# RoPE with scaled positions on one core: storing unit 0 from its fp16 tile by four casting DMAs, without ScalarE's copies

## The chip, the cores and the metric

One core of a Trainium2 chip. The metric is the device time of one execution in microseconds (us); a kernel's time is the median of its runs. "Span" is the length of the one profiled execution, which is some 1.7 us shorter than the timed figure. All runs quoted here are in the fast state. Each ratio is the mean time of one kernel's fast runs over the mean of the other's in the same rounds, so it is not quite the ratio of the medians beside it. A transfer (DMA) is carried by 16 DMA engines in packets, here mostly one row of one partition each; the trace keeps a record of every packet (start, duration, bytes), and on each engine one of 4 bytes that reports the completion of a DMA.

## The reference

```python
x: (8, 8, 1024, 64) float32; freqs: (32,); positions: (1024,); scale 0.5
angles = np.outer(positions * scale, freqs)
cos, sin = np.cos(angles), np.sin(angles)
x_first, x_second = x[..., :32], x[..., 32:]
out_first  = x_first * cos - x_second * sin
out_second = x_first * sin + x_second * cos
return np.concatenate([out_first, out_second], axis=-1).astype(np.float32)
```

16.8 MB of fp32 are read and 16.8 MB of fp32 are written. Little arithmetic stands against these bytes.

## The kernel before

The 64 (batch, head) pairs are four units of 16; a unit is a tile of 128 partitions by N = 8192 elements, that is 4 MB of fp32 or 2 MB of fp16. NH is half a row. Units are loaded by GpSimd's queue, which casts fp32 to fp16 on the way (half of unit 0 comes as fp32 by SyncE's and ScalarE's queues, to start early). VectorE computes in fp16, in place; ScalarE copies each half unit to an fp32 tile; units 0 and 1 are stored by GpSimd's queue, units 2 and 3 by SyncE's.

```python
# loads on GpSimd's queue (fp32 in memory, fp16 tiles); unit 0's second half was loaded above
pin(nc.gpsimd.dma_start(out=Xf[0][:, :NH], in_=xv[0][:, :NH]))
# ... constants ...
for u in range(1, NU):
    c = C2 if u == NU - 1 else 0                      # C2 = 1024: the last load is split
    pin(nc.gpsimd.dma_start(out=Xf[u][:, : N - c], in_=xv[u][:, : N - c]))
    if c:
        pin(nc.gpsimd.dma_start(out=Xf[u][:, N - c :], in_=xv[u][:, N - c :]))
# ... table of sin and cos (T), by TensorE and ScalarE; cut ...
for u in range(NU):
    OUT = xout.tile([P, N], FP32, tag="O")            # three buffers
    for s in range(2):                                # halves of the row
        # ... pr = Xs * sin; Xs = Xs * cos; Xs.first -= pr.second; Xs.second += pr.first (VectorE)
        pin(nc.scalar.copy(out=OUT[:, ns], in_=Xf[u][:, ns]))
        if u >= NU // 2:
            pin(nc.sync.dma_start(out=ov[u][:, ns], in_=OUT[:, ns]))
    if u < NU // 2:
        c = C1 if u == 0 else 0                       # C1 = 512
        if c:
            pin(nc.gpsimd.dma_start(out=ov[u][:, :c], in_=OUT[:, :c]))
        pin(nc.gpsimd.dma_start(out=ov[u][:, c:], in_=OUT[:, c:]))
```

## Time and profile before

| | before |
|---|---|
| time, median of 3 runs | 84.4 us (84.38 to 84.5) |
| span | 82.7 us |
| VectorE busy | 60.3 us (73%) |
| ScalarE busy | 40.1 us (49%) |
| memory read and written | 16.79 + 16.78 MB |

The prediction below shows the slices, queues, stretches and waits. Two groups of the page belong to the change. The columns are line, engine, operation, output<-input with its shape, count; then busy us and mean ns of one; then the engine's idle time before them and what ended it.

```profile
L165 ACT CAST OUT<-X 128x4096 f32<-128x4096 f16 x8 | 28.8, 3605 | 24.2 <-DVE X L162 24.2
...
L172 POOL DMA_DIRECT2D out_dram<-OUT x2 | 1.1, 531 | 20.2 <-ACT OUT L165 20.2
```

The eight copies are the fp32 outputs, 3.6 us each, and all of ScalarE's waits before them are for VectorE. GpSimd's store issues in turn wait for the copies.

### The profile page before, as it was taken

How to read it: one execution, taken by the hardware profiler on the slowest of the kernel's cores; microseconds unless marked ns; L12 is line 12 of the kernel's file. 1: busy time of each engine (PE TensorE's matmuls, PEld its weight loads, DVE VectorE, ACT ScalarE, POOL GpSimd, SP SyncE). 2: the span in 40 equal slices, each digit the busy share in tenths (PEclk: the TensorE clock that was granted, in tenths of full speed). 3: DMA queues.
4: the chain of work that ended last, by engine and by line, in shares of the span. 5: the costliest groups of instructions: out<-in, count | busy, mean ns of one | idle time of the engine just before them, and what ended most of it. 6: DMA issues, size and time to landing. Idle time of an engine off the chain costs nothing.

```text
span 82.7 us, 184 instructions
## 1 busy us (share of the span) xinstructions
PE 6.4 (8%) x18; PEld 2.4 (3%) x18; DVE 60.3 (73%) x40; ACT 40.1 (49%) x18; POOL 5.7 (7%) x16
## 2 busy tenths in 40 slices
PE   0011798200000000000000000000000000000000
PEld 0011232000000000000000000000000000000000
DVE  0306276999999999999999999999999997000000
ACT  0602159999960691294089049309705912950000
POOL 4950000000020002000000200000000000000000
PEclk9999999995555555555555555555555555555555
DMA  3899998996998999999499889989899899999991
GB/s 55 323 323 269 297 325 186 254 254 135 246 254 182 198 254 222 222 222 222 36 456 446 357 386 476 507 357 460 380 523 404 365 428 428 460 404 436 428 428 79
DMA packets 2099, 26.22 MB, mean 317 GB/s; under 512 B 371, under 2 KB 371, under 8 KB 563
## 3 DMA queue, kind: packets, MB, share of 16 engines
q0 software_dynamic: 1088, 15.73, 66.7%
q1 hardware_dynamic: 720, 9.44, 27.3%
q10 hardware_dynamic: 290, 1.06, 3.2%
q14 instruction: 1, 0.00, 0.0%
HBM read 16.79 MB, written 16.78 MB: 406 GB/s over the span
## 4 chain that ended last, share of the span: by engine, by line
DVE 54%; ACT 14%; issue 7%; DMA 6%; PE 5%; DVEq 1%; ACTq 0%
DVE X L158 19%; DVE pr L157 19%; DVE X L162 9%; DMA freq_row<-in_freqs_dram 6%; ACT T L144 5%; DVE X L159 5%; ACT OUT L165 4%; PE ps L134 4%; ACT X L145 4%; DVEq L203 1%; PE cfreq L102 1%; ACT tab L127 1%; DVE r L118 1%; DVE y L109 1%; ACTq L71 0%
## 5 line engine op out<-in xcount | busy, mean ns | idle before, releaser
L165 ACT CAST OUT<-X 128x4096 f32<-128x4096 f16 x8 | 28.8, 3605 | 24.2 <-DVE X L162 24.2
L157 DVE TENSOR_TENSOR pr<-X,T 128x4096 f16<-128x4096 f16 x8 | 18.3, 2292 | 1.0 <-ACT T L144 0.7
L158 DVE TENSOR_TENSOR X<-X,T 128x4096 f16<-128x4096 f16 x8 | 18.3, 2292 | 0.3
L159 DVE TENSOR_TENSOR X<-X,pr 128x2048 f16<-128x2048 f16 x8 | 9.8, 1225 | 0.3
L162 DVE TENSOR_TENSOR X<-pr,X 128x2048 f16<-128x2048 f16 x8 | 9.7, 1218 | 0.0
L144 ACT CAST T<-ps 128x1024 f16<-128x1024 f32 x6 | 5.7, 1030 | 2.6 <-PE ps L134 2.6
L134 PE MATMUL ps<-tab,sel 128*128 128x512 f16 x16 | 5.8, 503 | 2.6 <-ACT tab L127 2.2
L142 DVE CAST T<-ps 128x1024 f16<-128x1024 f32 x2 | 2.4, 1224 | 2.2 <-PE ps L134 2.2
L145 ACT CAST X<-X0f 128x4096 f16<-128x4096 f32 x1 | 3.6, 3650 | 0.0
L100 DVE COPY sel<-one 128x2048 f16<-128x2048 f16 x1 | 0.7, 694 | 2.8 <-POOL one L89 2.8
L122 ACT ACTIVATE tab<-r 128x256 f16<-128x256 f32 x1 | 0.4, 416 | 4.4 <-DVE r L118 4.4
L172 POOL DMA_DIRECT2D out_dram<-OUT x2 | 1.1, 531 | 20.2 <-ACT OUT L165 20.2
L122 ACT ACT_TABLE_LOAD x1 | 1.3, 1283 | 2.1 <-issue 2.1
L134 PEld LDWEIGHTS <-sel 128*128 128x128 f16 x16 | 1.9, 122 | 6.1 <-issue 5.7
L95 POOL DMA_DIRECT2D X<-in_x_dram x3 | 2.0, 658 | 0.0
L171 POOL DMA_DIRECT2D out_dram<-OUT x1 | 0.6, 554 | 19.1 <-ACT OUT L165 19.1
L105 DVE CAST posf<-pos_i 128x8 f32<-128x8 int32 x1 | 0.2, 173 | 2.2 <-DMA pos_i<-in_positions_dram 2.2
L102 PE MATMUL cfreq<-freq_row,coef 1*128 1x32 f32 x2 | 0.6, 391 | 5.9 <-DMA freq_row<-in_freqs_dram 5.9
L109 DVE TENSOR_TENSOR y<-posf,cfreq 128x256 f32<-128x256 f32 x1 | 0.4, 420 | 0.7 <-PE cfreq L102 0.7
L85 POOL DMA_DIRECT2D X<-in_x_dram x1 | 0.7, 669 | 0.8 <-POOLq L189 0.8
L102 PEld LDWEIGHTS cfreq<-freq_row,coef 1*128 1x128 f32 x2 | 0.5, 308 | 5.9 <-issue 5.9
L97 POOL DMA_DIRECT2D X<-in_x_dram x1 | 0.6, 557 | 0.0
(12 smaller groups left out, 2.8 us busy)
## 6 DMA issues: line engine op xcount, KB each, us to landing
out_dram<-OUT SPq DMA_DIRECT2D x4, 2048.0 KB, 11.6
X<-in_x_dram POOLq DMA_DIRECT2D x2, 2048.0 KB, 24.2
out_dram<-OUT POOLq DMA_DIRECT2D x1, 4096.0 KB, 20.4
out_dram<-OUT POOLq DMA_DIRECT2D x1, 3840.0 KB, 21.1
X<-in_x_dram POOLq DMA_DIRECT2D x1, 1792.0 KB, 37.5
X0f<-in_x_dram SPq DMA_DIRECT2D x1, 1024.0 KB, 4.7
X<-in_x_dram POOLq DMA_DIRECT2D x1, 1024.0 KB, 11.5
X0f<-in_x_dram ACTq DMA_DIRECT2D x1, 1024.0 KB, 13.4
```

Of the source, the lines that this page charges most:

```text
L95: pin(nc.gpsimd.dma_start(out=Xf[u][:, : N - c], in_=xv[u][:, : N - c]))
L102: nc.tensor.matmul(out=cfreq, lhsT=coef, rhs=freq_row, start=True, stop=True)
L122: pin(nc.scalar.activation(out=tab[:, 0], in_=r, func=AF.Sin, bias=0.0, scale=-_TWO_PI_DN))
L134: nc.tensor.matmul(out=ps[:, i].rearrange("p t w -> p (t w)"), lhsT=sel[:, g + i].rearrange("s h q -> s (h q)"), rhs=tab.rearrange("s t k ...
L142: pin(nc.vector.tensor_copy(out=dst, in_=ps))
L144: pin(nc.scalar.copy(out=dst, in_=ps))
L145: pin(nc.scalar.copy(out=Xf[0][:, NH:], in_=X0f[:, :NH]))
L157: pin(nc.vector.tensor_tensor(out=pr, in0=Xs, in1=sin_b, op=ALU.mult))
L158: pin(nc.vector.tensor_tensor(out=Xs, in0=Xs, in1=cos_b, op=ALU.mult))
L159: pin(nc.vector.tensor_tensor(out=Xs[:, :, 0, :], in0=Xs[:, :, 0, :], in1=pr[:, :, 1, :], op=ALU.subtract))
L162: pin(nc.vector.tensor_tensor(out=Xs[:, :, 1, :], in0=pr[:, :, 0, :], in1=Xs[:, :, 1, :], op=ALU.add))
L165: pin(nc.scalar.copy(out=OUT[:, ns], in_=Xf[u][:, ns]))
```

## The change

The intent: take unit 0's two copies off ScalarE. GpSimd's queue can cast while it stores, so unit 0 goes from its fp16 tile to fp32 memory directly, in four DMAs of 2048 elements a row (8 KB at the fp32 end).

```diff
--- before.py
+++ after.py
@@ -45,7 +45,6 @@
     K8 = S // P
     G = P // HP
     W = K8 * half
-    C1 = 512
     C2 = 1024
     assert S % HP == 0 and D == 2 * half and NBH % HEADS == 0 and G * K8 == K
 
@@ -145,8 +144,11 @@
     pin(nc.scalar.copy(out=Xf[0][:, NH:], in_=X0f[:, :NH]))
 
 
+
     for u in range(NU):
-        OUT = xout.tile([P, N], FP32, tag="O")
+        OUT = Xf[0]
+        if u:
+            OUT = xout.tile([P, N], FP32, tag="O")
         for s in range(2):
             ks = slice(s * KH, (s + 1) * KH)
             ns = slice(s * NH, (s + 1) * NH)
@@ -162,14 +164,15 @@
             pin(nc.vector.tensor_tensor(
                 out=Xs[:, :, 1, :], in0=pr[:, :, 0, :], in1=Xs[:, :, 1, :], op=ALU.add
             ))
-            pin(nc.scalar.copy(out=OUT[:, ns], in_=Xf[u][:, ns]))
+            if u:
+                pin(nc.scalar.copy(out=OUT[:, ns], in_=Xf[u][:, ns]))
             if u >= NU // 2:
                 pin(nc.sync.dma_start(out=ov[u][:, ns], in_=OUT[:, ns]))
         if u < NU // 2:
-            c = C1 if u == 0 else 0
-            if c:
-                pin(nc.gpsimd.dma_start(out=ov[u][:, :c], in_=OUT[:, :c]))
-            pin(nc.gpsimd.dma_start(out=ov[u][:, c:], in_=OUT[:, c:]))
+            parts = 4 if u == 0 else 1
+            for i in range(parts):
+                c = slice(i * N // parts, (i + 1) * N // parts)
+                pin(nc.gpsimd.dma_start(out=ov[u][:, c], in_=OUT[:, c]))
 
 
 # ---- launch: one core; inputs and outputs as the reference has them ----
```

## The prediction

> **What bounds the kernel now.** I read the page first (slices, queues), then the stretches, then the chain and the waits, to see whether an engine or the transfers set the end. The page's slices and its queue table:
>
> ```profile
> DVE  0306276999999999999999999999999997000000
> ACT  0602159999960691294089049309705912950000
> DMA  3899998996998999999499889989899899999991
> q0 software_dynamic: 1088, 15.73, 66.7%
> q1 hardware_dynamic: 720, 9.44, 27.3%
> q10 hardware_dynamic: 290, 1.06, 3.2%
> HBM read 16.79 MB, written 16.78 MB: 406 GB/s over the span
> ```
>
> DMA stands near 9 from the second slice to the last but one, that is before, beside and after VectorE's row, while ScalarE's row is full of holes. The dips (6, 4) look like idle time, so I looked closer. The stretches (last two columns: DMA share, GB/s):
>
> ```profile
> 17.00:29.00 12.00, 0.00 (x0) 0.00 (x0) 11.72 (x8) 8.39 (x4) 0.55 (x1) 0.58 1.02 218
> 29.00:40.00 11.00, 0.00 (x0) 0.00 (x0) 10.83 (x7) 5.85 (x2) 0.53 (x1) 0.50 1.05 214
> 40.00:43.00 3.00, 0.00 (x0) 0.00 (x0) 2.97 (x3) 1.32 (x1) 0.00 (x0) 0.50 0.98 228
> 43.00:53.00 10.00, 0.00 (x0) 0.00 (x0) 9.86 (x6) 5.89 (x2) 0.53 (x1) 0.50 1.00 430
> 53.00:73.00 20.00, 0.00 (x0) 0.00 (x0) 16.59 (x11) 10.35 (x3) 0.00 (x0) 0.50 1.01 433
> 73.00:81.00 8.00, 0.00 (x0) 0.00 (x0) 0.00 (x0) 0.47 (x1) 0.00 (x0) 0.50 0.99 426
> ```
>
> In windows longer than a packet the share is 1: the dips are packets counted whole at their start. Laying the single packet records of the trace end to end confirms it: from 2.2 to 81.3 us some 16 data packets are always open, one for each engine. The GB/s count the bytes that are written: a casting load writes half of what it reads, so 218 is 436 GB/s at the fp32 end, and the plain stores' 430 to 433 are the same speed. So the fp32 bytes of a packet set its duration, cast or not. The queue table agrees: on q0, 15.73 MB hold 7.34 MB of fp16 from 14.68 MB of fp32, so 23.07 fp32 MB in 66.7% of 16 x 82.7 us, which is 26.1 GB/s for each engine; q1, all plain, has 9.44 MB in 27.3%, 26.1 too.
>
> Is there a second bound close behind? The chain that ended last, and what SyncE and GpSimd waited for:
>
> ```profile
> 65.14 2.30 DVE X L158
> 67.45 0.02 issue
> 67.47 1.22 DVE X L159
> 68.69 1.15 DVEq L203
> 69.84 0.02 issue
> 69.86 3.60 ACT OUT L165
> ```
> ```profile
> SPq L167 <- ACT OUT L165: 71.3, 4, 51.2
> ```
> ```profile
> POOL out_dram L171 <- ACT OUT L165: 19.1, 1, 19.1
> ```
>
> VectorE runs without a hole from 13.4 to 69.8 us, then ScalarE's last copy ends at 73.46 and the last 2 MB store is issued at 73.5. It lands 8.3 us later (smallest value of the fp32 tile's issue-to-landing times), at 81.8. That store alone needs 8 packets per engine x 0.611 us = 4.9 us; an early 1 MB load shows what comes on top: it landed in 4.7 us with 8 x 0.309 = 2.5 us of packets, so 2.2 us. Hence about 73.5 + 7.1 = 80.6 us without a backlog, and the backlog is worth 1.2 us. The end is set by the DMA engines, with the VectorE chain 1.2 us behind.
>
> **What the Trainium skill says.** "DMA: Bandwidth & Descriptors", section "Where 436 GB/s comes from", gives 435 GB/s for the 16 engines; the trace shows 430 to 436, so there is nothing left to win in rate. The same page, "Queues, rings and completion order", says that an engine takes one ring's descriptors in order and turns between rings packet by packet; here unit 0's first piece is issued at 24.3 us but lands 19.3 us later, behind the loads in GpSimd's queue. "Why small descriptors are slow (HBM only)" tells of a fixed overhead per packet; the plain packets here took 0.309 us for 8 KB, 0.611 for 16 KB and 1.213 for 32 KB, some 0.01 us each beyond the bytes. "SBUF — State Buffer", section "Who interferes with whom", says that tensor_tensor does not stall GpSimd's writing of descriptors (marked as inferred); VectorE's products take 2291 to 2293 ns beside all of GpSimd's issues, so I expect no interference.
>
> **The change, part by part.**
>
> *Removed: two ScalarE copies* of 3.605 us (at 20.42 and 27.64), 7.2 of its 40.1 us. Who waited for them? Only GpSimd's two issues of unit 0. ScalarE's next copy, at 34.6, starts when VectorE's L162 is done, and still will. Nothing on VectorE's chain moves: worth 0 directly.
>
> *Moved: the issues of unit 0.* The first two parts can go when VectorE ends the first half, 19.17 + 1.22 = 20.4 us instead of 24.3; the other two at about 27.6 instead of 31.5. But q0 works in order, and in the packet records its last load ends at 42.6; unit 0's first packet started at 42.2. All four parts will queue behind the loads as now: 3.9 us earlier at the issue, 0 at the transfer.
>
> *Moved: buffers.* The output pool has three slots, one held by the early fp32 half of unit 0. Before, unit 3 took unit 0's slot, whose last store landed at 52.6, 10 us before unit 3's first copy at 62.86; afterwards it takes the slot free since 20.5 us. No wait was there, none goes. The second unit's store still waits for its own copies and is issued at 45.6.
>
> *Changed: the packets of unit 0.* This is all that is left on the bound. Before, each engine had 8 packets of 30 KB at 1.138 us and 4 of 4 KB (two 2 KB rows in one) at 0.159: 9.10 + 0.64 = 9.74 us, seen as 42.2 to 52.3. After, four DMAs of 128 rows give 4 x 8 = 32 packets an engine with 8 KB at the fp32 end. At the plain rate of 0.310 us: 9.92 us, +0.18. A cast may add something: casting loads took 1.227 us for 32 KB read against 1.213 plain, 0.014 more; 32 x 0.324 = 10.37 us, +0.63. But in the casting stretch 16.3 packets are open at a time instead of 16.1, so most of the 0.014 overlaps with the next packet. I take +0.25 us. It delays unit 1's packets and, as the backlog never empties, all stores after them up to the last.
>
> *The turn from loads to stores.* Around 39 to 41 us the last load packets take up to 2.24 us instead of 1.076, and the 2 KB ones 0.233 on average instead of 0.173: about 1 us lost for each engine (0.5 + 0.5). I don't know the cause, and the change replaces the small packets just after it; this could go either way by half a microsecond. I leave it at 0.
>
> Sum: 84.4 + 0 + 0 + 0.25 = 84.65, rounded to 84.6 us.
>
> **The rivals.**
> 1. *The casting store is slower than the plain one at the same fp32 bytes.* No casting store is in the profile; only casting loads. If an engine were bound by its elements or by reads of 4 KB, 10% more on 9.7 us would be +1 us (85.4), and slower by 2% (86.1) needs 17%. For it: the direction is untried here. Against it: the loads show the cast hidden at full rate.
> 2. *The earlier issue or the finer rows help*: a shorter turn from loads to stores, up to 1 us, and the floor at 80.6 us caps any such gain at 1.2 us, so 83.2 at best. For it: the lost microsecond at 40 us. Against it: it lies in the loads' packets, which the change leaves alone.
> 3. *ScalarE was a bound and 7.2 us come free.* It idles 24.2 us for VectorE; I give this nothing.
> 4. *Smaller packets on q0 lose their share against SyncE's 16 KB packets.* Queues share by packets, and unit 0 would get less; but unit 0 is through at 52.3 and SyncE's first packet starts at 55.8. And total work is unchanged.
>
> **Range and chances.** The sure term is +0.2, the cast's up to +0.6, the turn plus or minus 0.5: 84.0 to 85.3 us. Faster by over 2% (below 82.7) is beyond the floor unless VectorE's chain itself shortens: 0.02. Slower by over 2% needs casting stores at least 17% slower: 0.07. Within 2%: 0.91.
>
> **What would show it.** Right: VectorE's last L162 still ends near 69.8 us and the last store is issued near 73.5; ScalarE shows 6 copies at 3.605 us, about 33 us busy; GpSimd's first store issue near 20.5; q0 with 320 more packets and about the same share; DMA share still 1.0 from 43 to 81 us, and 420 to 430 GB/s between 43 and 53. Wrong: fewer GB/s in that stretch (rival 1), first stores under way clearly before 42 us or a shorter turn (rival 2), or a VectorE chain that ends earlier, which I have no reason for.

## The result, and the profile after

The changed kernel takes 84.59 us (6 runs, 84.52 to 84.68), the kernel before 84.42 us in the same rounds (6 runs). The ratio is 1.0018, with an interval of 1.0005 to 1.0031: a difference of under 2%, yet a slowdown of about 0.15 us that the interval keeps away from zero.

The page's slices and queue table of the changed kernel (packets, MB, share of 16 engines):

```profile
DVE  0306376999999999999999999999999996000000
ACT  0603169998000000393098059219607903940000
...
DMA  3899997996999899999499999979999799999991
...
q0 software_dynamic: 1440, 15.73, 68.2%
q1 hardware_dynamic: 720, 9.44, 27.3%
q10 hardware_dynamic: 290, 1.06, 3.2%
```

ScalarE's row is now empty in slices 10 to 15, counted from 0, where the two copies were, and DMA's row is as full as before. q0 has 352 more packets: 320 for data (32 instead of 12 on each of 16 engines), and 32 completions, since two more DMAs report from 16 engines each.

The groups that the change touches:

```profile
L168 ACT CAST OUT<-X 128x4096 f32<-128x4096 f16 x6 | 21.6, 3606 | 31.3 <-DVE X L164 31.3
...
L175 POOL DMA_DIRECT2D out_dram<-X x4 | 2.1, 538 | 21.7 <-DVE X L164 21.7
```

Two copies of 3.6 us are gone (28.8 to 21.6), and ScalarE's wait for VectorE grew by 7.1 us (24.2 to 31.3): the freed time became idle time, to the microsecond. The stores now wait for VectorE itself.

The stretches (busy us and instructions of PE, PEld, DVE, ACT and POOL, then the granted clock; the last two columns are DMA share and GB/s written):

```profile
40.00:43.00 3.00, 0.00 (x0) 0.00 (x0) 2.97 (x3) 1.48 (x1) 0.00 (x0) 0.50 0.93 194
43.00:53.00 10.00, 0.00 (x0) 0.00 (x0) 9.86 (x6) 5.73 (x2) 0.53 (x1) 0.50 1.14 440
53.00:73.00 20.00, 0.00 (x0) 0.00 (x0) 16.43 (x11) 10.51 (x3) 0.00 (x0) 0.50 1.00 431
73.00:81.00 8.00, 0.00 (x0) 0.00 (x0) 0.00 (x0) 0.31 (x1) 0.00 (x0) 0.50 1.00 430
```

Unit 0 is written between 42 and 52 us. The share of 1.14 there looks like 14% more work, but the rate fell by only 1%: a casting store of 8 KB is on record for 0.341 us against 0.309 for the plain 8 KB load of before, and the records overlap, with 18 of them open at a time on 16 engines. The share above 1 is an overlap of records and no measure of cost. (440 against 430 is mostly edge: packets are counted whole where they start. With each packet's bytes laid evenly over its record, 44 to 51.5 us has 428 GB/s here and 433 in the kernel before.)

The end of the chain that ended last (start, us, what), and SyncE's wait (us in total, times, longest):

```profile
67.31 1.22 DVE X L161
68.53 1.15 DVEq L206
69.68 0.02 issue
69.70 3.60 ACT OUT L168
```
```profile
SPq L170 <- ACT OUT L168: 71.1, 4, 51.1
```

VectorE's chain is where it was (it ended 0.16 us earlier in this execution, because the frequencies landed earlier), and the last store is issued at 73.3 us. In the packet records unit 1's last packet ends at 65.14 us instead of 65.03, and the last packet of all at 81.55 instead of 81.45. So the delay enters with unit 0 and is carried to the end, although the last store was issued 0.16 us earlier. These are single executions, and the changed kernel's second profile ends at 81.50; the spacing of the packets, shown after the experiments with 2 KB rows, is steadier.

### The profile page after: what moved, and what is told of

The parts are those of the page before. It is cut to its first block, busy times and chain, and to the rows that moved or that the text cites. A ratio compares the mean times of both kernels' runs of the same rounds, so it can differ in the third digit from the quotient of the medians.

```text
span 82.8 us, 184 instructions
## 1 busy us (share of the span) xinstructions
PE 6.5 (8%) x18; PEld 2.5 (3%) x18; DVE 60.3 (73%) x40; ACT 33.0 (40%) x16; POOL 6.7 (8%) x18
## 3 DMA queue, kind: packets, MB, share of 16 engines
q0 software_dynamic: 1440, 15.73, 68.2%
## 4 chain that ended last, share of the span: by engine, by line
DVE 54%; ACT 15%; issue 7%; DMA 5%; PE 5%; DVEq 1%; ACTq 0%
DVE X L160 19%; DVE pr L159 19%; DVE X L164 9%; ACT T L143 6%; DMA freq_row<-in_freqs_dram 5%; DVE X L161 5%; ACT OUT L168 4%; PE ps L133 4%; ACT X L144 4%; DVEq L206 1%; PE cfreq L101 1%; ACT tab L126 1%; DVE r L117 1%; DVE y L108 1%; ACTq L70 0%
## 5 line engine op out<-in xcount | busy, mean ns | idle before, releaser
L168 ACT CAST OUT<-X 128x4096 f32<-128x4096 f16 x6 | 21.6, 3606 | 31.3 <-DVE X L164 31.3
L175 POOL DMA_DIRECT2D out_dram<-X x4 | 2.1, 538 | 21.7 <-DVE X L164 21.7
L175 POOL DMA_DIRECT2D out_dram<-OUT x1 | 0.5, 533 | 16.4 <-ACT OUT L168 16.4
## 6 DMA issues: line engine op xcount, KB each, us to landing
X<-in_x_dram POOLq DMA_DIRECT2D x2, 2048.0 KB, 24.2
```

Of the source, the lines that this page charges most:

```text
L175: pin(nc.gpsimd.dma_start(out=ov[u][:, c], in_=OUT[:, c]))
```

## The experiments

Theory A is the prediction's: the DMA engines are full from 2 to 81 us, a packet costs its bytes at the fp32 end plus a small fixed time, a cast costs nothing, and ScalarE's copies are off the path. The rivals: B, the cast itself costs; C, the freed ScalarE or the earlier issue wins something that fine rows lose again; D, casting loads and casting stores could overlap inside an engine; and one that holds the compute chain to set the end. All kernels below gave correct results. One of the kernel before's eleven runs beside the first four kernels (whole, plain 8 KB, 2 KB, copies kept) took 85.08 us; without it their ratios would be 0.0006 higher.

### One casting store with rows of 32 KB

```diff
-            parts = 4 if u == 0 else 1
+            parts = 1
```

> Unit 0 in one casting store with rows of 32 KB: 8 packets an engine instead of 32. Theory A (the engines are full, a packet costs its fp32 bytes plus about 0.01 us, a cast costs nothing): 0.2 us under the changed kernel, so 84.35 to 84.45, level with the kernel before. Rival B (it is the cast that costs, not the rows): no better than the changed kernel, 84.6 or more. Rival C (the earlier issue wins something and the fine rows lose more): clearly under the kernel before, 84.2 or less.

Measured: 84.5 us, ratio to the kernel before 0.9995 (0.9974 to 1.0017). The same kernel was run again beside the changed kernel itself, unedited:

> The changed kernel once more, unedited, in the same rounds as the next two, so that a few tenths can be compared. Theory A: 84.6, 1.001 to 1.003 of the kernel before.

> The one casting store with rows of 32 KB again, beside the changed kernel: theory A (cost by packets) has it 0.1 to 0.2 us below the changed kernel and level with the kernel before; rival B (cost of the cast) level with the changed kernel.

Measured: the changed kernel 84.51 us, ratio 1.0015 (1.0003 to 1.0028); the single casting store 84.41 us, ratio 0.9995 (0.9982 to 1.0009). Its queue row, from the first of its two runs:

```profile
q0 software_dynamic: 1008, 15.73, 67.1%
```

With the same cast and the same copies gone, but 8 packets an engine instead of 32 and one DMA instead of four, the 0.15 us are gone (in the second call all five runs, 84.33 to 84.46, lie below the changed kernel's five, 84.49 to 84.70). That speaks against B. It also speaks against C: with rows as long as before there should have been a gain, and there is none.

### The old cut, cast

```diff
-            parts = 4 if u == 0 else 1
-            for i in range(parts):
-                c = slice(i * N // parts, (i + 1) * N // parts)
+            cuts = (0, 512, N) if u == 0 else (0, N)
+            for lo, hi in zip(cuts, cuts[1:]):
+                c = slice(lo, hi)
```

> Unit 0 cast in the store, but cut as in the kernel before (512 elements of a row, then the other 7680): the same packets at the fp32 end, 8 of 30 KB and 4 of 4 KB an engine, so the cast alone. Theory A: level with the kernel before within 0.1 us, 84.4 to 84.5. Rival B: like the changed kernel, 84.6.

Measured, in the same rounds as the two above: 84.43 us against 84.45, ratio 1.0002 (0.999 to 1.0015). This is the cast alone, with the kernel before's cut of the rows: it costs nothing that can be measured, at most 0.13 us by the interval. One detail was not as expected: the two 2 KB rows that a plain store puts into one packet stay two packets when they are cast (128 packets of 2 KB in place of 64 of 4 KB).

### Rows of 8 KB without a cast

```diff
-        OUT = Xf[0]
-        if u:
+        if True:
             OUT = xout.tile([P, N], FP32, tag="O")
...
-            if u:
+            if True:
                 pin(nc.scalar.copy(out=OUT[:, ns], in_=Xf[u][:, ns]))
```

> Unit 0 is copied by ScalarE to fp32 as before, and stored without a cast in four DMAs with rows of 8 KB: the row size alone. Theory A: 84.6, like the changed kernel. Rival B (the cast costs): 84.4, like the kernel before. Rival C (earlier issue and free ScalarE win, rows lose): above the changed kernel, 84.8.

Measured: 84.68 us, ratio 1.0018 (0.9994 to 1.0042). Its queue row, and the stretch in which unit 0 is written:

```profile
q0 software_dynamic: 1440, 15.73, 66.9%
```
```profile
43.00:53.00 10.00, 0.00 (x0) 0.00 (x0) 9.83 (x7) 5.42 (x2) 0.53 (x1) 0.50 1.05 445
```

The ratio is the changed kernel's (1.0018), though nothing is cast here and ScalarE works as before. By itself this run cannot tell 84.6 from 84.4, as its interval holds both; with the kernels above it fits the finer cut and not the cast. It also shows how little the queue's share is worth as a measure of cost: the same packets have 66.9% here and 68.2% when they are cast, and the cast kernel is not slower.

### Rows of 2 KB

```diff
-            parts = 4 if u == 0 else 1
+            parts = 16 if u == 0 else 1
```

> Unit 0 in sixteen casting stores with rows of 2 KB: the suspected cost per packet enlarged. Theory A: 64 packets of 4 KB an engine if two rows go into one packet, 52 more than before at 0.009 us, 84.9; 128 packets of 2 KB if they don't, 85.4. Rival B (a cast costs by its bytes): 84.6, like the changed kernel.

Measured: 84.91 us, ratio 1.0044 (1.0022 to 1.0066). Queue row and stretch:

```profile
q0 software_dynamic: 3168, 15.73, 72.6%
```
```profile
43.00:53.00 10.00, 0.00 (x0) 0.00 (x0) 9.86 (x6) 5.71 (x2) 5.30 (x10) 0.50 1.51 438
```

A finer cut costs more, as A has it and B does not. But A's size was wrong. The packets stayed at 2 KB, 128 an engine, for which A expected 85.4. The 116 packets more than before cost 0.0044 x 84.5 = 0.37 us, or 3.2 ns each and not 9. The share of 1.51 shows why the sum of durations misled: each is on record for 0.115 us, but some 1.4 to 1.5 times as many as there are engines are open at a time. The rate did suffer, though the view's 438 hides it by counting unit 1's first packets whole: from 44 to 51.5 us, where unit 0 alone is moved, it is 408 GB/s. GpSimd spent 5.3 us of the stretch on issues; before them it waited for earlier transfers to land.

The packet records show what the cut costs. On each engine, the time from the completion of the last load to that of unit 0's last store (mean of the 16 engines, one profile a kernel unless marked) is:

| unit 0's store | DMAs | packets an engine | us | against before |
|---|---|---|---|---|
| plain, 2 KB + 30 KB rows (before) | 2 | 12 | 9.716 | |
| cast, the old cut | 2 | 16 | 9.698 | -0.02 |
| cast, 32 KB rows (both runs) | 1 | 8 | 9.658 | -0.06 |
| cast, 8 KB rows (the change, both runs) | 4 | 32 | 9.778 | +0.06 |
| plain, 8 KB rows | 4 | 32 | 9.822 | +0.11 |
| cast, 2 KB rows | 16 | 128 | 10.258 | +0.54 |

A cast row costs no more than a plain one: casting packets of 30 KB follow each other every 1.132 us against 1.134 plain, and those of 8 KB every 0.304 against 0.306. The finer cut has two costs, which the times alone do not part. A cast packet is spaced 1207.2 ns at 32 KB, 303.7 at 8 KB and 77.8 at 2 KB, so each packet adds about 2.5 ns to its bytes; and from one completion to the next, a further casting DMA adds 20 ns on each engine (2449.4 ns for the second to fourth part, 2429.5 for the first), a further plain one about 7 (2452.9 against 8 packets at 305.8). From the whole store to the change that is 24 x 2.5 + 3 x 20 = 120 ns, half packets and half DMAs. From unit 0's end to the last packet all are nearly alike: 29.31 us before, 29.33 to 29.40 in the others. The 2 KB kernel's loads happened to be through 0.2 us earlier than the kernel before's in the profiles (42.21 against 42.42 us, mean of the engines), so its 0.37 us, and the 3.2 ns taken from them, are no clean price of a packet.

### ScalarE's copies put back, read by nobody

```diff
-        OUT = Xf[0]
-        if u:
-            OUT = xout.tile([P, N], FP32, tag="O")
+        OUT = xout.tile([P, N], FP32, tag="O")
...
-            if u:
+            if True:
                 pin(nc.scalar.copy(out=OUT[:, ns], in_=Xf[u][:, ns]))
...
-                pin(nc.gpsimd.dma_start(out=ov[u][:, c], in_=OUT[:, c]))
+                pin(nc.gpsimd.dma_start(out=ov[u][:, c], in_=(OUT if u else Xf[0])[:, c]))
```

> The changed kernel with ScalarE's two copies of unit 0 put back; they go to a buffer that nothing reads. Theory A: 84.6, the same as the changed kernel within 0.1 us, ScalarE 40 us busy again. Rival C (7.2 us of ScalarE are worth something): above it by 0.2 us or more.

Measured: 84.64 us, ratio 1.0013 (0.9989 to 1.0038). Its first part of the page:

```profile
PE 7.0 (8%) x18; PEld 2.7 (3%) x18; DVE 60.3 (73%) x40; ACT 40.1 (48%) x18; POOL 6.7 (8%) x18
```

ScalarE is 40.1 us busy again, and the ratio does not rise over the changed kernel's. 7.2 us of ScalarE are worth nothing in this place that the interval, some 0.2 us each way, can show.

### Every store cast, no output copies at all

```diff
-        OUT = Xf[0]
-        if u:
-            OUT = xout.tile([P, N], FP32, tag="O")
+        OUT = Xf[u]
...
-            if u:
-                pin(nc.scalar.copy(out=OUT[:, ns], in_=Xf[u][:, ns]))
             if u >= NU // 2:
-                pin(nc.sync.dma_start(out=ov[u][:, ns], in_=OUT[:, ns]))
+                pin(nc.gpsimd.dma_start(out=ov[u][:, ns], in_=OUT[:, ns]))
...
-            parts = 4 if u == 0 else 1
+            parts = 1
```

> Every unit is stored from its fp16 tile by GpSimd's casting queue, units 0 and 1 whole, units 2 and 3 in halves; ScalarE copies no output at all, so that the last store can be issued 3.6 us earlier, near 70 us. Theory A (the DMA engines are full to the end, the chain of VectorE and ScalarE runs 1.2 us behind them): level with the kernel before, 84.3 to 84.6, and the last store's landing takes some 3.5 us longer instead. Rival (the chain VectorE, ScalarE, last store sets the end): some 3 us faster, 81.5.

Measured: 84.88 us against 84.52, ratio 1.0054 (1.0037 to 1.007). GpSimd's last issue, from its timeline (start, us, what, idle before it), and the last stretches:

```profile
69.89 0.53 POOL L166 DMA_DIRECT2D out_dram<-X  x1 [6.51 <-DVE X L162]
```
```profile
70.00:81.00 11.00, 0.00 (x0) 0.00 (x0) 0.00 (x0) 0.00 (x0) 0.42 (x1) 0.50 1.06 429
81.00:83.00 2.00, 0.00 (x0) 0.00 (x0) 0.00 (x0) 0.00 (x0) 0.00 (x0) 0.50 0.02 0
```

This is the strongest evidence for the bound. The last store is issued at 69.9 us instead of 73.5, and the program ends no earlier: that store takes 11.9 us to land instead of 8.3 (the smallest issue-to-landing times of the two kernels' stores), the 3.6 us that it was early. From 70 to 81 us the engines write 429 GB/s without a VectorE or ScalarE instruction beside them, and the last packet ends at 81.45 us, as in the kernel before. The chain of computation does not set the end.

It is 0.4 us slower, outside what A gave. The packets end at the same time as before but the span is 83.0 us, not 82.7: 0.3 us lie after the last packet, where the last store is now GpSimd's and not SyncE's. The trace shows where: after the last landing SyncE passes five semaphore instructions (81.84 to 82.09 us) in place of one at 81.81. Why they come so late was not tested.

### Loads and casting stores in turn

```diff
-    for u in range(1, NU):
-        c = C2 if u == NU - 1 else 0
+    for u in range(1, NU - 1):
+        c = 0
...
-            parts = 4 if u == 0 else 1
+            parts = 8 if u == 0 else 1
             for i in range(parts):
                 c = slice(i * N // parts, (i + 1) * N // parts)
                 pin(nc.gpsimd.dma_start(out=ov[u][:, c], in_=OUT[:, c]))
+                if u == 0:
+                    v = NU - 1
+                    pin(nc.gpsimd.dma_start(out=Xf[v][:, c], in_=xv[v][:, c]))
```

> Unit 0's casting store and unit 3's casting load are cut into eight pieces each and issued in turn on GpSimd's queue, so that fp16 is read and fp32 written by one packet while fp32 is read and fp16 written by the next. Theory A in its strict form (a packet holds its engine for its fp32 bytes, whatever its direction): no gain; 64 packets of 4 KB instead of 32 of 8 KB for the store, and as many for the load, at 0.009 us: 85.0. Rival D (an engine's reads and its writes overlap between packets, so that a casting load beside a casting store saves up to a quarter of their 19 us): the stretch from 32 to 52 us is shortened by 1 to 4 us, and the time falls to 83.4, where VectorE's chain holds it.

Measured: 85.08 us, ratio 1.007 (1.0057 to 1.0082), near A's 85.0 (though by 0.009 us a packet, a price that the 2 KB rows refuted). The same 20 us of this kernel and then of the changed kernel, in which unit 3 is loaded and unit 0 is stored in both:

```profile
32.50:52.50 20.00, 0.00 (x0) 0.00 (x0) 19.73 (x12) 10.82 (x3) 5.34 (x10) 0.50 1.21 327
```
```profile
32.50:52.50 20.00, 0.00 (x0) 0.00 (x0) 19.73 (x12) 10.82 (x3) 0.53 (x1) 0.50 1.11 329
```

327 and 329 GB/s: nothing is gained by turning between the directions at a grain of eight packets an engine. Rival D falls for this grain. A finer turn was not tried, so that is left open.

### The last load whole

```diff
-        c = C2 if u == NU - 1 else 0
+        c = 0
```

> The changed kernel without the split of the last load (unit 3 comes in one DMA with rows of 32 KB): is the microsecond lost at the turn from loads to stores that of the small load's packets? If it is: 83.6 to 84.0. If the loss stays with the last load packets whatever their size: 84.5 to 84.7.

Measured: 84.74 us, ratio 1.0024 (1.0012 to 1.0036), 0.04 us above what was expected if the loss stays. The loss at the turn from loads to stores is not the small load's: without it 29 packets of the last 16 KB (fp16) rows took 1.31 to 2.24 us instead of 1.227, all started between 38.8 and 40.8 us, together 1.1 us for each engine. (Unlike the share of 1.14, this is lost rate: with the bytes laid evenly over the records, the kernel before moves 346, 213 and 319 GB/s in the three us from 39 to 42, against 433 around them.) In the kernel where loads and stores alternate, the slow packets lie at 29 to 31 us, ahead of its first store, which comes earlier there. So the loss seems to go with the first turn from loads to stores, wherever it comes. What causes it stays open.

No kernel here beats both: the best, the single casting store, is level with the kernel before (0.9995 both times, and both intervals hold 1).

## Why the prediction was right

The time was predicted as 84.6 us and is 84.59. By its steps:

- *What bounds it.* Right, and shown by the store that was issued 3.6 us early and took 3.6 us longer to land. The prediction's "1.2 us" for the distance of the VectorE chain was not tested: no kernel made the transfers shorter. It is soft too: the early load that it is taken from had packets of 0.374 us on average, slow ones of up to 1.09 us among them, and not 0.309; with that the sum gives some 1.7 us.
- *ScalarE's copies, worth 0.* Right: put back, they changed nothing.
- *The earlier issue, worth 0.* Right. The first part was issued at 20.5 us, and the four parts took up to 26.8 us to land. The longer wait behind the loads took back what the issue had won.
- *Buffers.* Right as far as seen: ScalarE's waits before its copies remain VectorE's.
- *The packets, +0.25 us.* Right in sign, and too high: about +0.15 us by the times (1.0018 and 1.0015, with intervals from 0.03 to 0.26 us), 0.06 us by the spacing of unit 0's packets. Its two sources were told apart: the cast adds nothing measurable (1.0002), and the finer cut accounts for what the records show; whether the rest of the 0.15 us is more than noise is not shown. The "+0.18" and the 0.01 us a packet were read from durations, which overlap: the spacing gives 2.5 ns a cast packet. The prediction left out the number of DMAs: row size and DMAs were changed together in every run, but the spacing parts them, and half of what the four rows of 8 KB cost over one of 32 KB is the three further DMAs.
- *The turn from loads to stores, 0.* Right by luck as much as by reasoning: the loss stayed at about 1 us in both kernels (0.97 us an engine in either, from the packets' excess over their medians). Its cause is open.
- *Signs to look for.* Three did not come as stated. "About the same share" of q0 was 1.5 points higher, and the DMA share of 1.0 between 43 and 53 us was 1.14: a casting store's record is longer (0.341 against 0.309 us) and overlaps its neighbours. The rate there was 440 GB/s by the view and not 420 to 430, by the edge of the window; laid evenly it is 428. And the count of 320 more packets left out 32 completions.
- *The range.* Its terms add to 84.1 to 85.5 us, not to the 84.0 to 85.3 that it gives. The result lies in both.

## What to carry to other kernels

Where the transfer engines are full from end to end, as here, taking work off a compute engine, or issuing a store earlier, only moved waiting from one place to another; count the bytes at the wide end of each packet, and see whether they change. A cast moved into a store was free in time here, so it can buy back an engine or a buffer, but keep its rows long and its DMAs few: cut for a reason, not by habit. Check a busy share against the rate before calling it cost, since overlapping records inflate it; and for a difference of 1%, measure the spacing of packets, since a window that counts packets whole is wrong by more at its edges.

## What the Trainium skill lacked or had wrong

- "DMA: Bandwidth & Descriptors" (section "SWDGE vs HWDGE vs iDMA") says which queue can cast, but not what a cast costs. Here a casting load of 32 KB fp32 is on record for 1.227 us and a plain store of 32 KB for 1.213, casting and plain stretches both move some 430 GB/s at the fp32 end, and a store with the cast and the same cut took 1.0002 of the time without it, its 30 KB packets 1.132 us apart instead of 1.134.
- The same page (section "Why small descriptors are slow (HBM only)") gives about 3 cycles of overhead a packet, and no time in that section. The spacing of cast packets here gives about 2.5 ns a packet (1207.2 ns for 32 KB, 303.7 for 8 KB, 77.8 for 2 KB), and 20 ns more on each engine for each further casting DMA.
- No page that I read tells that a load queue's last packets slow down ahead of the first store: 0.7 to 1.2 us lost an engine in all twelve profiles, at some 39 to 42 us or, with an earlier first store, at 29 to 31 us.
- No page that I read says by how much DMA packet records overlap: shares of 1.12 and 1.47 stood beside 428 and 408 GB/s from 44 to 51.5 us, where the kernel before moves 433 (laid evenly): shares 12% and 47% above 1 went with 1% and 6% less rate.
